# Products of 1024 columns from two PSUM banks, and attention scores in the projections' banks

## The chip, the cores and the metric

The kernel runs on one core of one Trainium2 chip. The metric is the time of one execution on the device, in microseconds (us). A core has five engines that work side by side, each through its own instructions in order: TensorE (PE, matmuls; its weight loads are shown apart as PEld), VectorE (DVE), ScalarE (ACT), GpSimd (POOL) and SyncE (SP), which here issues the loads. Matmuls write to PSUM, which this kernel uses as eight banks of 128 partitions by 512 fp32 columns.

## The reference

Two layers act on 256 latent tokens of width 2048, with 256 context tokens beside them; all is fp32. From the conditioning vector c each layer makes a shift, a scale and a gate, three vectors of 2048 values, with one large matrix (2048 by 6144 per layer). Cut to what matters here:

```python
sc = silu(c)
for layer in range(2):
    mod = sc @ ada_w[layer] + ada_b[layer]           # 6144 values
    shift, scale, gate = split(mod, 3)
    h = rmsnorm(x, norm_g[layer]) * (1 + scale) + shift
    if layer == 0:
        k, v, q, za, glu, zb = split(h @ w_in)       # context tokens give k and v too
        q, k = rope(rmsnorm(q)), rope(rmsnorm(k))    # 8 query heads, 2 key/value heads, 128 wide
        s = q @ k.T * 128 ** -0.5                    # 256 queries, 512 keys
        attn = softmax(s) @ v
        conv = silu(layernorm(depthwise_conv_31(glu)))
        x = x + gate * (concat(attn * silu(za), conv * silu(zb)) @ w_out)
    else:
        u, v, z = split(h @ od_w_in)                 # gated position mixing
        x = x + gate * ((gelu(u) * mix(layernorm(gelu(v))) * silu(z)) @ od_w_out)
out = rmsnorm(x, final_g)
```

## The kernel before, in words

**Jobs.** All weights are streamed from memory once, in blocks of 128 partitions by up to 1024 columns (512 KB). A block is a job: its load goes to one of ten ring buffers (tag `raw`), 12 jobs ahead of its use. A weight job is then split into a high and a low part, the high one by ACT (L358), the low one by POOL or VectorE (L361), and enters matmuls in three products (L383, L385, L386 where features lie on partitions; L406 to L408 where tokens do) that accumulate in one PSUM bank. A gate projection (`z_part`) has four groups of 96 such matmuls; ACT takes each out of its bank with a SiLU (L588). There are two gate projections, z0 and z1.

**The conditioning vectors.** One part of `ada_w` goes over TensorE. For eight blocks of 1024 output columns (TSET), c alone is needed, and these go over VectorE, in `adat_jobs`: the matrix is stored transposed, output columns on partitions, and a job multiplies a block elementwise with c and sums along the row (L269, a product with an accumulator; the trace shows the accumulator's read as an operation of its own). c, copied over all partitions, lies in SBUF as `cb` (2048 columns); `cb_part` has ACT copy 512 columns of it to a PSUM bank (`cbp`, L248), from which VectorE reads it. A block has 16 jobs in four column ranges q of 512; each job holds two sets of 128 output columns (k = 0, 1) and makes two products of 512 columns. After four jobs ACT fills the bank with the next range. Blocks run through the ranges alternately upwards and downwards, so that one filling serves two of them. The partial sums land in `res` and are added by L277. Four of the eight blocks are used in layer 0's stretch of the program, four in layer 1's.

**PSUM.** Every tile in PSUM is one bank with a tag: three banks for the projections' accumulators (`acc`, tag a), one for the attention scores (`S`, tag s), one for `cbp` (tag c), and three for everything else (tag m: the convolution, the transposes, the attention output and the sums).

**Attention.** For each of 16 heads and query blocks, `attn_head` makes the scores in S (L755, 128 queries by 512 keys), VectorE takes the maximum from S (L758), ACT the exponential from S (L761), VectorE scales the result (L766). `attn_tr` transposes it on TensorE (L775), `attn_pv` multiplies four heads with the values (L783), and ACT copies that out (L787). S is held from its matmul to the end of its exponential. The convolution's 31 taps per channel block are VectorE operations into PSUM (L613).

**The order.** The program lists the jobs in a plan; conditioning jobs are woven between weight jobs, and the steps of attention and convolution are handed out after each weight job at a set pace. The scheduler of the language then orders each engine's instructions by their place in the program and by a simulation of their times; a tile gets a bank when one of its tag is free in that simulation. On the chip every engine keeps that order, and waits at the instruction whose inputs or bank are not ready.

Of the kernel before, what the change touches and what calls it, by code (L numbers as in the profile page):

```python
# [11 lines left out]
F32 = mybir.dt.float32  # L12
F32R = mybir.dt.float32r
AF = mybir.ActivationFunctionType
ALU = mybir.AluOpType
AX = mybir.AxisListType

D = 2048
NKB = 16
T = 256  # L20
# [15 lines left out]
SMALL_W = _off  # L36
BANKS = {"acc": "a", "S": "s", "conv": "m", "ada": "m", "cbp": "c"}
BUFS = {'a': 3, 's': 1, 'm': 3, 'c': 1}
ZG = ()
# [20 lines left out]
RW = 10  # L60
# [22 lines left out]
def backbone_kernel(  # L83
# [21 lines left out]
    nc = tc.nc  # L105
# [8 lines left out]
    def ld(dst, src):  # L114
        """a load, in the order of the program."""
        i = nc.sync.dma_start(dst, src)
        cnt[0] += 1
        return tc.keep_in_program_order(i) if cnt[0] <= NL else i
# [46 lines left out]
    def bcast(dst, n, hi=rowh, lo=rowl, k=10):  # L165
        """row n over all partitions; dst in PSUM."""
        nc.tensor.matmul(dst, sel[0:k, n : n + 1].broadcast_to([k, 128]), hi, start=True, stop=False)
        nc.tensor.matmul(dst, sel[0:k, n : n + 1].broadcast_to([k, 128]), lo, start=False, stop=True)
# [16 lines left out]
    def colsum(p, ones, src, n, tot):  # L185
        """partial sums over the partitions of block n of tot, in the column tile n % 4 of the PE array."""
        g = n % 4
        nc.tensor.matmul(p[32 * g : 32 * g + 32, :T], ones, src, start=n < 4, stop=n >= tot - 4, tile_position=(0, 32 * g))  # L188

    def colsum_all(p):  # L190
        """the four partial sums added, on every partition, in PSUM."""
        r = tmp.tile([128, T], F32, tag="adar", name="csum", bufs=1)
        nc.scalar.copy(r, p[:, :T])
        o = bank("csum_p")
        nc.tensor.matmul(o[:, :T], q4, r, start=True, stop=True)
        return o

    def colsum_rstd(p):
        """1 / sqrt(the four partial sums added + eps) of each token, on every partition, in PSUM."""
        r = tmp.tile([128, T], F32, tag="adar", name="csum", bufs=1)  # L200
# [14 lines left out]
    def warm(func):  # L215
        """loads the table of func ahead of its use."""
        tc.keep_in_program_order(nc.scalar.activation(wrm, epsc, func))
# [12 lines left out]

# [1 line left out]
    modv = [con.tile([128, 3, NKB], F32, name=f"modv{i}") for i in range(2)]  # L232
    modc = con.tile([128, 2, NKB], F32, name="modc")

    class Job:
        raw = None
# [7 lines left out]
    def cb_part(q):  # L244
        """columns 512 q .. of cb to PSUM."""
        if cbq["q"] != q:
            cbq["q"], cbq["t"] = q, bank("cbp")
            nc.scalar.copy(cbq["t"], cb[:, q * 512 : (q + 1) * 512])  # L248

    def adat_jobs(l, c0):  # L250
        """1024 columns for c alone, columns on partitions, on the vector engine."""
        js = []
        n = TSET.index((l, c0))
        res = tmp.tile([128, 8, 4], F32, tag="adat", name="adat", bufs=2)
        order = range(4) if n % 2 == 0 else range(3, -1, -1)
        for u, q in enumerate(order):
            for t in range(4):
                jb = Job()
                jb.kind = "A"

                def load(jb=jb, t=t, q=q):
                    jb.raw = ring.tile([128, 2, 512], F32, tag="raw", name="traw", bufs=RW)
                    ld(jb.raw, adat_d[n, q, t].rearrange("p (a b) -> p a b", a=2))

                def mm(jb=jb, t=t, q=q, u=u):
                    cb_part(q)
                    with after("crit"):
                        for k in range(2):
                            nc.vector.scalar_tensor_tensor(  # L269
                                out=jb.raw[:, k, :], in0=jb.raw[:, k, :], scalar=1.0, in1=cbq["t"], op0=ALU.mult,  # L270
                                op1=ALU.mult, accum_out=res[:, 2 * t + k, q : q + 1])
                    if t == 3 and u < 3:
                        cb_part(order[u + 1])
                    if t == 3 and u == 3:
                        kind, k0 = c0 // D, (c0 % D) // 128
# [10 lines left out]
    def adan_jobs(l, c0, cw, slot=1):  # L286
        """columns c0 .. c0 + cw of a layer's adaLN projection, four column tiles of the PE array at a time;
        rows 32 g and 32 g + 1 of the result are c and c_ctx, for a part of the columns (or of the k-blocks)."""
        js = []
# [52 lines left out]

# [1 line left out]
    def w_job(src, width, mmf, tot=1024):  # L344
        """src: [128, tot] block in DRAM, width: columns of a k-row."""
        jb = Job()
# [20 lines left out]
    def w_rows(jobs, src, kbs, h, post):  # L367
        """features on partitions: [128 of 2 blocks, tokens]; src[kq] is the block of 4 k-blocks."""
        accs = {}
# [21 lines left out]
    def w_cols(jobs, src_f, kbs, hs, post):  # L391
        """tokens on partitions: hs = list of (h, chunk); src_f(kp) gives the block of 2 k-blocks."""
        parts = [(kp, [kb % 2 for kb in kbs if kb // 2 == kp]) for kp in sorted({kb // 2 for kb in kbs})]
# [26 lines left out]

# [1 line left out]
    def rms_rB(src_half, name):  # L422
        """rstd of each token over D, broadcast over partitions."""
        pr = bank("rms")
        for i in range(2):
            sq = s8("sq")
            nc.scalar.activation(sq, src_half[i], AF.Square)
            if i == 1:
                warm(AF.Sqrt)
            for k in range(8):  # L430
                colsum(pr, onesD, sq[:, k, :], i * 8 + k, 16)
        rB = tmp.tile([128, T], F32, tag="rB", name=name, bufs=2)
        nc.scalar.copy(rB, colsum_rstd(pr))
        return rB
# [5 lines left out]
    def make_h(src_f, rB, shift, scale, hh, hl, kbs, m=8, rP=None, mh=0):  # L440
        """hh/hl [128, 8, T] pieces for the k-blocks kbs (2 at a time)."""
        prev = None
# [20 lines left out]

# [1 line left out]
    zT = {}  # L465
# [43 lines left out]
    def weave(a, b):  # L509
        """b spread evenly through a."""  # L510
        out, n = [], 0
# [12 lines left out]
    def part(dst, a, g):  # L524
        """partial sum over a K group into dst."""
        if g == 0:
# [4 lines left out]
    def kv_part(kqs):  # L531
        """keys (cg 0) and values (cg 1) of x and of the context over some K: [128 tokens of two chunks, 256]."""
        js = [hook(lambda kq=kq: prep_c(kq)) for kq in kqs]
# [42 lines left out]
    def z_part(which, g=None):  # L576
        """SiLU gates; over one K group when g is given, else over all of K."""
        js = []
# [16 lines left out]

# [1 line left out]
    TAPS = [PAD] + [t for t in range(CW) if t != PAD]  # L597

    def conv_taps(i, t0, t1):
        """taps t0 .. t1 (of TAPS) of channel block i; the first covers every token."""  # L600
        if i % 2 == 0 and t0 == 0:
# [69 lines left out]

# [1 line left out]
    knb = con.tile([128, 128], F32, name="knb")  # L673
# [18 lines left out]
    def rope(dst, src, nm, c, nh):  # L692
        """dst, src: [128, nh, 128] (even half, odd half)."""
        def tb(n):
# [23 lines left out]
    def rope_k(i):  # L718
        """rows of keys: chunks 0,1 latent (rotated), 2,3 context."""
        if "kT" not in at:  # L720
# [87 lines left out]

# [1 line left out]
    def hm(kb):  # L810
# [3 lines left out]
    def out_part(w, l, h, fin, kbs, last):  # L814
        """x += gate * (h @ w) over the k-blocks kbs."""
        segs = []
# [14 lines left out]

# [1 line left out]
    l1 = {}  # L833
# [35 lines left out]
    def v_part(g):  # L869
        """half the K of v; with the second half its statistics and norm."""  # L870
        js = []
# [40 lines left out]
    def sgu(i):  # L912
        """mixed positions of channel blocks 2i, 2i+1 (one group) times u."""
        pm = bank("sgu")
# [63 lines left out]

# [1 line left out]
    def need(key):  # L980
# [112 lines left out]
def _layout(i):  # L1093
# [25 lines left out]
    def xt(x):  # L1119
# [6 lines left out]
        "ada": np.concatenate([a["ada_w"][l][:, c : c + 256] for l, c in NCOLS], axis=1),  # L1126
        "adat": np.stack([a["ada_w"][l][:, c : c + 1024].T.reshape(4, 2, 128, 4, 512).transpose(3, 0, 2, 1, 4).reshape(4, 4, 128, 1024)
                          for l, c in TSET]),
# [23 lines left out]
```

## Time and profile before

| | |
|---|---|
| time, median of 3 runs | 936.31 us (932.75 to 938.0) |
| profiled execution: its span | 928.0 us, first to last instruction |
| median of the runs less that span | 8.3 us |
| TensorE busy in the span | 869.7 us (94%) |
| VectorE busy | 684.8 us (74%) |
| ScalarE busy | 456.1 us (49%) |
| GpSimd busy | 256.1 us (28%) |
| read from memory | 235.80 MB, 256 GB/s over the span |
| mean granted TensorE clock | 0.979 of full speed |

The profile is of one execution; its span leaves out what lies before the first and after the last instruction. Lines of groups read: source line, engine, operation, output<-inputs by the program's names with their shapes, count | busy us, mean ns of one | idle time of the engine just before them, and what ended most of it. Lines in order of time begin with the start and the duration in us; a bracket at the end tells how long the engine had stood idle and what released it. Lines of stretches give the stretch, its length, each engine's busy time with the number of instructions, the granted clock, the DMA share and GB/s.

### The profile page before, as it was taken

The numbers are of one execution on the slowest core, as the hardware profiler recorded it, in microseconds if no ns is written. First come the engines' busy times: TensorE is split into PE (matmuls) and PEld (weight loads), VectorE is DVE, ScalarE is ACT, GpSimd is POOL, SyncE is SP. The second block draws the span as 40 slices with busy tenths as digits, with TensorE's granted clock in tenths as the row PEclk, the third lists the DMA queues.
The fourth block names the chain that finished last, engine by engine and source line by source line (L and its number), as shares of the span: only waits on it lengthen the run. The fifth ranks groups of instructions, "written<-read, shape, count | busy, mean of one in ns | idle before, by whom it ended". The sixth has DMA issues, their size and how long they took to land.

```text
span 928.0 us, 17854 instructions
## 1 busy us (share of the span) xinstructions
PE 869.7 (94%) x7052; PEld 793.0 (85%) x7052; DVE 684.8 (74%) x1432; ACT 456.1 (49%) x650; POOL 256.1 (28%) x111
## 2 busy tenths in 40 slices
PE   5899999898987999998989899999999999999995
PEld 3788999897766987788979778998899999999994
DVE  1365565889999999987796289889989877654443
ACT  4544132464644755554654454555474444444441
POOL 0000014567856544556687630000000000000000
PEclk9899999999989999999999999999999999999998
DMA  9999989855776844667869689998987888755502
GB/s 320 374 387 354 332 300 360 315 205 142 244 275 203 281 151 135 221 199 236 300 227 367 207 289 399 375 333 287 312 304 228 252 273 273 229 183 176 165 1 90
DMA packets 79152, 239.05 MB, mean 258 GB/s; under 512 B 7503, under 2 KB 15961, under 8 KB 78557
## 3 DMA queue, kind: packets, MB, share of 16 engines
q1 hardware_dynamic: 79068, 237.92, 75.0%
q8 instruction: 55, 0.90, 0.4%
q14 instruction: 29, 0.23, 0.1%
HBM read 235.80 MB, written 2.10 MB: 256 GB/s over the span
## 4 chain that ended last, share of the span: by engine, by line
PE 51%; DVE 5%; DMA 2%; ACT 1%; issue 1%; POOL 0%; DVEq 0%; POOLq 0%
PE acc L386 13%; PE acc L385 13%; PE acc L383 12%; PE acc L406 3%; PE acc L407 3%; PE acc L408 3%; DMA traw<-adat 2%; DVE traw L269 1%; DVE conv L613 1%; PE rms L188 1%; PE sgu L918 1%; DVE P L766 1%; DVE gaT L645 1%; DVE mBl L438 1%; ACT whi L358 0%
## 5 line engine op out<-in xcount | busy, mean ns | idle before, releaser
L358 ACT ACTIVATE whi<-raw 128x1024 fp32r<-128x1024 f32 (+1 forms) x256 | 263.5, 1031 | 287.7 <-PE acc L385 131.9
L361 POOL TENSOR_TENSOR wlo<-raw,whi 128x1024 fp32r<-128x1024 f32 x104 | 254.9, 2459 | 293.8 <-ACT whi L358 280.7
L361 DVE TENSOR_TENSOR wlo<-raw,whi 128x1024 fp32r<-128x1024 f32 (+1 forms) x152 | 176.9, 1165 | 103.6 <-ACT whi L358 102.7
L269 DVE SCALAR_TENSOR_TENSOR traw<-traw,cbp 128x512 f32<-128x512 f32 x256 | 165.0, 680 | 37.3 <-DMA traw<-adat 30.6
L383 PE MATMUL acc<-h,whi 128*128 128x256 f32 x512 | 150.6, 296 | 1.9 <-ACT h L453 1.9
L385 PE MATMUL acc<-h,whi 128*128 128x256 f32 x512 | 150.4, 295 | 1.9 <-DVE h L457 1.9
L386 PE MATMUL acc<-h,wlo 128*128 128x256 f32 x512 | 146.9, 288 | 0.0
L383 PE MATMUL acc<-h1h,whi 128*128 128x256 f32 x512 | 145.3, 284 | 0.0
L385 PE MATMUL acc<-h1l,whi 128*128 128x256 f32 x512 | 144.9, 283 | 0.0
L386 PE MATMUL acc<-h1h,wlo 128*128 128x256 f32 x512 | 144.6, 283 | 0.0
L613 DVE SCALAR_TENSOR_TENSOR conv<-gaT,small,conv 128x242 f32<-128x242 f32 (+14 forms) x240 | 107.7, 472 | 1.8
L383 PEld LDWEIGHTS acc<-h,whi 128*128 128x128 f32 x512 | 99.0, 194 | 8.2 <-issue 3.7
L385 PEld LDWEIGHTS acc<-h,whi 128*128 128x128 f32 x512 | 99.1, 194 | 6.6 <-issue 4.0
L386 PEld LDWEIGHTS acc<-h,wlo 128*128 128x128 f32 x512 | 99.0, 194 | 3.5 <-issue 3.5
L383 PEld LDWEIGHTS acc<-h1h,whi 128*128 128x128 f32 x512 | 98.2, 192 | 0.1
L385 PEld LDWEIGHTS acc<-h1l,whi 128*128 128x128 f32 x512 | 98.3, 192 | 0.1
L386 PEld LDWEIGHTS acc<-h1h,wlo 128*128 128x128 f32 x512 | 98.1, 192 | 0.0
L386 PE MATMUL acc<-m1h,wlo 128*128 128x256 f32 x256 | 73.1, 286 | 0.0
L383 PE MATMUL acc<-m1h,whi 128*128 128x256 f32 x256 | 72.4, 283 | 0.0
L385 PE MATMUL acc<-m1l,whi 128*128 128x256 f32 x256 | 72.4, 283 | 0.0
L386 PEld LDWEIGHTS acc<-m1h,wlo 128*128 128x128 f32 x256 | 49.1, 192 | 2.9 <-issue 2.9
L407 PE MATMUL acc<-wlo,h1h 128*128 128x512 f32 x128 | 50.7, 396 | 0.0
(230 smaller groups left out, 1667.5 us busy)
## 6 DMA issues: line engine op xcount, KB each, us to landing
traw<-adat SPq DMA_DIRECT2D x128, 512.0 KB, 4.7
raw<-w_out SPq DMA_DIRECT2D x64, 512.0 KB, 4.3
raw<-w_uz SPq DMA_DIRECT2D x64, 512.0 KB, 4.7
araw<-ada SPq DMA_DIRECT2D x56, 512.0 KB, 7.7
raw<-w_gate SPq DMA_DIRECT2D x56, 512.0 KB, 5.0
raw<-w_v SPq DMA_DIRECT2D x32, 512.0 KB, 5.2
raw<-w_q SPq DMA_DIRECT2D x16, 512.0 KB, 3.7
raw<-w_gate SPq DMA_DIRECT2D x16, 256.0 KB, 8.7
```

Of the source, the lines that this page charges most:

```text
L188: nc.tensor.matmul(p[32 * g : 32 * g + 32, :T], ones, src, start=n < 4, stop=n >= tot - 4, tile_position=(0, 32 * g))
L269: nc.vector.scalar_tensor_tensor(out=jb.raw[:, k, :], in0=jb.raw[:, k, :], scalar=1.0, in1=cbq["t"], op0=ALU.mult, op1=ALU.mult, accum_out ...
L358: nc.scalar.activation(hv, jb.raw, AF.Copy)
L361: eng.tensor_tensor(out=jb.lo.rearrange("p a b -> p (a b)"), in0=jb.raw, in1=hv.bitcast(F32), op=ALU.subtract)
L383: nc.tensor.matmul(o, wh, hh, start=(n == 0 and kt == kts[0] and b == 0), stop=False, skip_group_check=True)
L385: nc.tensor.matmul(o, wh, hl, start=False, stop=False, skip_group_check=True)
L386: nc.tensor.matmul(o, wl, hh, start=False, stop=end, skip_group_check=True)
L406: nc.tensor.matmul(accs[i], hh[:, sl], jb.hi[:, k, :], start=s0, stop=False)
L407: nc.tensor.matmul(accs[i], hh[:, sl], jb.lo[:, k, :], start=False, stop=False)
L408: nc.tensor.matmul(accs[i], hl[:, sl], jb.hi[:, k, :], start=False, stop=s1)
L438: return nc.vector.tensor_tensor(out=lo, in0=src, in1=hi.bitcast(F32), op=ALU.subtract)
L613: nc.vector.scalar_tensor_tensor(out=o, in0=y, scalar=w, in1=o, op0=ALU.mult, op1=ALU.add)
```

## The change

The layout of the eight transposed blocks on the host becomes two column ranges of 1024 with eight jobs each in place of four ranges of 512 with four; a job is the same 512 KB. `cbp` becomes a tile of two banks, filled by two copies of 512 columns, and a job is one product of 1024 columns. `res` has two partial sums per output in place of four. To free a bank, the tag s goes and S takes its bank from tag a, which keeps three. The diff without removed comments:

```diff
-BANKS = {"acc": "a", "S": "s", "conv": "m", "ada": "m", "cbp": "c"}
-BUFS = {'a': 3, 's': 1, 'm': 3, 'c': 1}
+BANKS = {"acc": "a", "S": "a", "conv": "m", "ada": "m", "cbp": "c"}
+BUFS = {'a': 3, 'm': 3, 'c': 1}
...
     def cb_part(q):
         if cbq["q"] != q:
-            cbq["q"], cbq["t"] = q, bank("cbp")
-            nc.scalar.copy(cbq["t"], cb[:, q * 512 : (q + 1) * 512])
+            cbq["q"], cbq["t"] = q, psum.tile([128, 1024], F32, tag="c", name="cbp", bufs=1)
+            for x in range(2):
+                nc.scalar.copy(cbq["t"][:, x * 512 : (x + 1) * 512], cb[:, q * 1024 + x * 512 : q * 1024 + (x + 1) * 512])
...
-        res = tmp.tile([128, 8, 4], F32, tag="adat", name="adat", bufs=2)
-        order = range(4) if n % 2 == 0 else range(3, -1, -1)
+        res = tmp.tile([128, 8, 2], F32, tag="adat", name="adat", bufs=2)
+        order = range(2) if n % 2 == 0 else range(1, -1, -1)
         for u, q in enumerate(order):
-            for t in range(4):
+            for t in range(8):
...
-                    jb.raw = ring.tile([128, 2, 512], F32, tag="raw", name="traw", bufs=RW)
-                    ld(jb.raw, adat_d[n, q, t].rearrange("p (a b) -> p a b", a=2))
+                    jb.raw = ring.tile([128, 1024], F32, tag="raw", name="traw", bufs=RW)
+                    ld(jb.raw, adat_d[n, q, t])
...
-                        for k in range(2):
-                            nc.vector.scalar_tensor_tensor(
-                                out=jb.raw[:, k, :], in0=jb.raw[:, k, :], scalar=1.0, in1=cbq["t"], op0=ALU.mult,
-                                op1=ALU.mult, accum_out=res[:, 2 * t + k, q : q + 1])
-                    if t == 3 and u < 3:
+                        nc.vector.scalar_tensor_tensor(
+                            out=jb.raw, in0=jb.raw, scalar=1.0, in1=cbq["t"], op0=ALU.mult,
+                            op1=ALU.mult, accum_out=res[:, t, q : q + 1])
+                    if t == 7 and u < 1:
                         cb_part(order[u + 1])
-                    if t == 3 and u == 3:
+                    if t == 7 and u == 1:
...
-        "adat": np.stack([a["ada_w"][l][:, c : c + 1024].T.reshape(4, 2, 128, 4, 512).transpose(3, 0, 2, 1, 4).reshape(4, 4, 128, 1024)
+        "adat": np.stack([a["ada_w"][l][:, c : c + 1024].T.reshape(8, 128, 2, 1024).transpose(2, 0, 1, 3)
                           for l, c in TSET]),
```

## The prediction

> **What bounds the kernel now.** I read the busy times of the page first, then the busy times of three long stretches, then the groups of VectorE, the waits, and the order of time where the scores are made. The page's span and first section:
>
> ```profile
> span 928.0 us, 17854 instructions
> ...
> PE 869.7 (94%) x7052; PEld 793.0 (85%) x7052; DVE 684.8 (74%) x1432; ACT 456.1 (49%) x650; POOL 256.1 (28%) x111
> ```
>
> TensorE (PE) is busy 94% of the span, so as a whole the kernel is bound by matmuls. VectorE (DVE), where the edit is, can move the end only in a stretch in which PE waits. Three stretches, with the columns PE, PEld, DVE, ACT, POOL, granted clock, DMA share and GB/s:
>
> ```profile
> 200.00:412.00 212.00, 192.65 (x1233) 167.05 (x1233) 203.79 (x476) 119.94 (x200) 127.00 (x53) 0.97 0.62 202
> 412.00:540.00 128.00, 118.71 (x897) 106.84 (x895) 86.82 (x200) 64.08 (x87) 83.26 (x35) 0.97 0.76 258
> 540.00:800.00 260.00, 259.98 (x1835) 244.45 (x1834) 223.43 (x444) 137.90 (x166) 6.81 (x3) 1.00 0.89 306
> ```
>
> From 540 to 800 us (layer 1) PE never stops. Whatever VectorE saves there is hidden by the matmuls. From 200 to 412 us (queries, rotary, attention, convolution taps) it is the other way round: VectorE is busy 203.8 of 212 us and PE shows 19 us of idle time. This stretch is where the edit is worth anything. From 412 to 540 us VectorE has 41 us of slack and PE 9.
>
> **The change part by part: the products.** A job of 512 KB is now two products of 512 columns; it becomes one of 1024. The groups of VectorE between 200 and 412 us, and the product's group between 412 and 540 us:
>
> ```profile
> L613 DVE SCALAR_TENSOR_TENSOR conv<-gaT,small,conv 128x242 f32<-128x242 f32 (+14 forms) x213 | 94.8, 472 | 1.3
> L269 DVE SCALAR_TENSOR_TENSOR traw<-traw,cbp 128x512 f32<-128x512 f32 x60 | 39.0, 677 | 1.7 <-DMA traw<-adat 1.0 <-ACT PT L776 0.7
> ```
> ```profile
> L269 DVE SCALAR_TENSOR_TENSOR traw<-traw,cbp 128x512 f32<-128x512 f32 x57 | 36.7, 681 | 19.2 <-DMA traw<-adat 16.1 <-issue 1.9 <-ACT whi L358 1.1
> ```
>
> 60 products are 30 jobs in the stretch that counts, and 57 are about 28 jobs in the next. What a product takes from its neighbours is the distance between starts, since the shown ends overlap the next start. VectorE in order of time, a job at 241 us and a 1024-column subtraction at 701 us:
>
> ```profile
> 241.34 0.68 DVE L269 SCALAR_TENSOR_TENSOR traw<-traw,cbp 128x512 f32<-128x512 f32 x1
> 241.94 0.08 DVE L269 DVE_READ_ACCUMULATOR traw<-traw,cbp 128x1 f32 x1
> 241.94 0.68 DVE L269 SCALAR_TENSOR_TENSOR traw<-traw,cbp 128x512 f32<-128x512 f32 x1
> ```
> ```profile
> 701.58 1.22 DVE L361 TENSOR_TENSOR wlo<-raw,whi 128x1024 fp32r<-128x1024 f32 x1
> 702.72 0.69 DVE L931 TENSOR_TENSOR m<-m,mixed 128x512 f32<-128x512 f32 x1
> ```
>
> Two products take 2 x 0.605 = 1.21 us. The accumulator's read starts with the next operation, so halving the number of reads gains nothing. No row shows a product of 1024 columns. It cannot be worse than two of 512 unless a read across two banks is slower, for which no row speaks: 1.21 us, no gain. The nearest row is the subtraction of the same width, 702.72 - 701.58 = 1.14 us. I take 1.135, so a job gains 0.075 us. In 200 to 412 us that is 30 x 0.075 = 2.2 us, all on the engine that bounds. In 412 to 540 us it is 28 x 0.075 = 2.1 us, but there VectorE stood 16.1 us waiting for the products' own loads, and a shorter product then only waits longer; I take half, 1.0 us. In layer 1 it is nothing, by the cover above; without that cover 61 jobs would be worth 4.6 us. Bounds of this part: 0 and 9.6 us (128 jobs).
>
> [...]
>
> **The conditioning copies and the loads.** ScalarE's (ACT's) group of copies over the whole span:
>
> ```profile
> L248 ACT COPY cbp<-cb 128x512 f32<-128x512 f32 x25 | 14.8, 592 | 22.4 <-DVE traw L269 22.4
> ```
>
> By the code the 25 fillings of one bank become 9 of two, so 18 copies of 0.59 us. ACT is busy 120 of 212 us, which covers them. Its waits for a product, which hold up what follows it on ACT, are in the waits between 200 and 420 us:
>
> ```profile
> ACT cbp L248 <- DVE traw L269: 12.5, 3, 8.8
> PE qtp L748 <- DVE qr L704: 12.2, 2, 6.8
> ```
>
> The 8.8 us wait lies beside a PE wait of 6.8 us for VectorE's rotary output (qr), which ACT does not feed, so taking it away releases nobody: 0, with up to 3 us if the shorter waits counted. Against it, the first product behind a switch now waits for two copies, 0.59 us more at each of 5 switches before 540 us: at most 3 us of loss. Loads stay 128 issues of 512 KB on SP's queue. I take 0 for all of it.
>
> **The scores.** S had a bank of its own; now it takes one of the three that the projections use. What the single bank costs: the scores' weight loads after 300 us, then PE and ACT in order of time.
>
> ```profile
> L755 PEld LDWEIGHTS S<-kT,qT x28: 186/192/192, 305.9 to 398.9; 128*128 128x128 f32 x28
> ```
> ```profile
> 308.37 0.28 PE L383 MATMUL acc<-h,whi 128*128 128x256 f32 x1
> ...
> 360.05 0.29 PE L383 MATMUL acc<-h,whi 128*128 128x256 f32 x1
> ...
> 368.18 1.13 PE L755 MATMUL S<-kT,qT 128*128 128x512 f32 x2 [1.22 <-ACT P L761]
> ...
> 378.42 0.28 PE L383 MATMUL acc<-h,whi 128*128 128x256 f32 x1
> ...
> 384.58 1.02 PE L755 MATMUL S<-kT,qT 128*128 128x512 f32 x2
> ```
> ```profile
> 310.11 0.60 ACT L588 ACTIVATE z0T<-acc 128x512 f32<-128x512 f32 x1
> ...
> 367.94 0.19 ACT L761 ACTIVATION_READ_ACCUMULATOR P<-S,mx,qss 128x1 f32 x1
> ...
> 382.00 0.19 ACT L761 ACTIVATION_READ_ACCUMULATOR P<-S,mx,qss 128x1 f32 x1
> ...
> 386.49 0.59 ACT L787 COPY mixA<-O 128x512 f32<-128x512 f32 x1 [3.35 <-PE O L783]
> ...
> 388.38 1.09 ACT L588 ACTIVATE z1T<-acc 128x512 f32<-128x512 f32 x2
> ```
>
> 28 loads are 14 heads, one every (398.9 - 305.9) / 13 = 7.1 us. The head at 368.18 starts as soon as the exponential before it is through with the bank (367.94 + 0.19). Where only one projection is open, S could now have a second bank. The wait of 1.22 us is the largest that PE shows there; I take it as gained once, 1.2 us (bounds 0 and the 6.9 us worked out below).
>
> What the missing bank costs: a gate group holds its bank through its 96 matmuls and then until ACT has made its SiLU. I counted groups of 96 from the first gate matmul: the third begins at 308.37, the sixth at 360.05, the seventh at 378.42. At 308.37 the first two gate groups wait for ACT (the earlier is out at 310.11 + 0.60) and a score is open, so all three banks would be taken: 2.3 us of wait. At 378.42 the groups before it are let go together at 388.38 + 1.09, because ACT's order puts them behind the third attention output (mixA at 386.49). The third bank then holds the score until 382.2, 3.8 us, and the score of 384.58 finds none until 389.0, 4.4 us. Behind a waiting matmul stands all of PE's order: more gate matmuls, the transposes of P, and behind these VectorE's maximum and ACT's exponential. Together 10.5 us. VectorE has taps and products queued meanwhile, and it is VectorE that bounds, so I take 3 us (bounds 0 and the 13.9 worked out below).
>
> **The sum.** -2.2 - 1.0 - 1.2 + 3 = -1.4 us. The profiled execution's span of 928.0 us lies 8.3 us below the median of the runs, 936.3; applied to the median, the sum gives 935, and I put 934, because the second bank's bound is open on the gaining side. The scheduler builds each engine's order from its own simulation, so operations will also change places. The price of that can only be bounded: VectorE's operations with two SBUF inputs do not take the same time everywhere.
>
> ```profile
> L701 DVE TENSOR_TENSOR qr<-rp,rp 128x256 f32<-128x256 f32 x4 | 6.3, 1582 | 0.0
> ```
>
> Four of one shape average 1.58 us, while 512 columns were shown at 0.68 to 0.69 in the rows above. So 4 us hang on where such a group falls. That makes about 5 us either way.
>
> **Rivals.** *Attention runs ahead (faster).* If S mostly has two banks, heads no longer follow one another at 7.1 us, the taps (94.8 us of VectorE) slide behind attention, where VectorE has its 41 us of slack, and PE's idle time there goes. Busy times:
>
> ```profile
> 280.00:300.00 20.00, 15.19 (x122) 14.51 (x121) 20.00 (x36) 8.88 (x13) 13.17 (x6) 0.96 0.59 188
> 300.00:320.00 20.00, 18.02 (x130) 17.09 (x131) 18.57 (x54) 13.04 (x19) 9.84 (x5) 0.87 0.88 308
> 300.00:420.00 120.00, 113.12 (x770) 96.32 (x770) 110.78 (x268) 71.93 (x103) 62.41 (x26) 0.98 0.61 201
> ```
>
> PE is idle 120 - 113.1 = 6.9 us from 300 to 420. With the products' 3.2 us that is 926 us. For it: the heads stand in a row behind one bank. Against it: VectorE is 110.8 of 120 us busy there and its order is fixed before the run, so a score that is early may only wait longer for its maximum.
>
> *The shared bank decides (slower).* All 10.5 us fall on PE's path, as the gate matmuls that PE cannot do before 420 us have to be done later, where it has little idle time. A PE wait like those for qr is followed by a lower clock: 0.96 and 0.87 in the two rows above, (0.04 + 0.13) x 20 = 3.4 us of lost matmul time. Then 10.5 + 3.4 - 3.2 gives about 947 us. It decides as soon as more than some 4 us of bank waits reach PE's path. For it: 29 us pass from the end of the fifth gate group, where the sixth begins (360.05), to its release at 389. Against it: the scheduler may start the gates' SiLU earlier when banks are short.
>
> [...]
>
> *The change does not shorten anything.* A product across two banks takes 1.21 us, or VectorE waits for loads instead: 936 us. This lies inside the forecast.
>
> **How the numbers follow.** The forecast, 934, has 0.46, with its own range 929 to 940. The faster rival has 0.30, the slower one 0.24. About 0.5% (4.7 us) is what a measurement of this kernel tells from no change. Of the forecast's 0.46, 0.34 lies within that, 0.07 below and 0.05 above. Of the faster rival 0.28 is below, of the slower one 0.22 above, and 0.02 of each within. That makes 0.35 faster, 0.38 the same, 0.27 slower. The range starts 6 us below the faster rival's price, about what the order may move, and ends at the slower one's, which has counted every wait in full: 920 to 947.
>
> **What would show it.** Products: 128 of 1024 columns, starts 1.13 to 1.14 us apart; 1.21 or more means no gain. Copies: 18, and fewer ACT waits for products. Scores: starts less than 7.1 us apart, with no start on the heels of an exponential, would be the faster rival. A PE wait for ACT's SiLU or exponential ahead of a gate matmul, or a clock below 0.95 between 300 and 420 us, would be the slower one. Layer 1, 540 to 800 us, should keep its length. If it doesn't, the prediction's cover is wrong. If attention ends more than 5 us from 412 us, my sum missed the main term.

## The result: 1.1% slower

The median after is 943.71 us (940.56 to 945.51) against 934.53 us for the kernel before beside it (931.3 to 939.48), six runs each. The ratio is 1.011, with a 95% interval of 1.0084 to 1.0136 (the two medians alone give 1.0098). Two of the twelve runs of one kernel below, before6_kr, were over 1.5% above its fastest, and its median and ratio leave them out. The forecast was 934 us with its own range up to 940. The time lies outside that, and inside the wide range that ended at 947.

The profiled execution of after has a span of 940.9 us and a time of 942.68 us. Its span is 12.9 us above that of before, while the medians are 9.2 us apart. So some 3.7 us of what the two traces show apart is the quick execution that was profiled before, and no reading below hangs on a difference that small.

The first section of after's page, then three stretches (columns PE, PEld, DVE, ACT, POOL, granted clock, DMA share, GB/s):

```profile
span 940.9 us, 17649 instructions
...
PE 880.5 (94%) x7052; PEld 799.6 (85%) x7052; DVE 683.9 (73%) x1176; ACT 453.4 (48%) x643; POOL 257.5 (27%) x111
```
```profile
200.00:412.00 212.00, 189.43 (x1143) 159.80 (x1143) 201.14 (x416) 116.52 (x196) 117.81 (x49) 0.94 0.55 183
412.00:540.00 128.00, 121.48 (x957) 111.79 (x956) 80.49 (x129) 62.11 (x81) 93.57 (x38) 0.99 0.80 279
540.00:800.00 260.00, 258.12 (x1756) 239.95 (x1757) 221.94 (x323) 134.51 (x163) 7.12 (x3) 0.98 0.87 298
```

Most of the loss lies between 200 and 412 us. PE's idle time there went from 212 - 192.65 = 19.3 to 212 - 189.43 = 22.6 us, which is 3.2 us. The granted clock fell from 0.97 to 0.94, which is about 0.03 x 212 = 6.4 us of full-speed matmul time. Together that is 9.6 us. From 412 to 800 us the same sum gives -0.9 us of idle time and, from the clocks, -2.6 + 5.2 us: some 2 us more. (The clocks are rounded to 0.01, so such a product can be off by some 2 us.)

The product itself did what was predicted. VectorE of after in order of time shows starts 1.14 us apart, where two halves took 1.21:

```profile
546.09 1.22 DVE L269 SCALAR_TENSOR_TENSOR traw<-traw,cbp 128x1024 f32<-128x1024 f32 x1
547.23 0.09 DVE L269 DVE_READ_ACCUMULATOR traw<-traw,cbp 128x1 f32 x1
547.23 1.22 DVE L269 SCALAR_TENSOR_TENSOR traw<-traw,cbp 128x1024 f32<-128x1024 f32 x1
```

So VectorE has less to do and PE waits longer for it. The larger waits of PE in after, 200 to 440 us (what waited, for what: us in total, times, longest):

```profile
PE qtp L748 <- DVE qss L221: 5.8, 2, 3.8
PE qtp L748 <- DVE qr L704: 3.7, 1, 3.7
PE ktp L735 <- DVE kr L732: 3.4, 1, 3.4
PE ktp L735 <- DVE kr L704: 3.2, 2, 2.0
PE qtp L748 <- DVE mx L762: 2.6, 1, 2.6
PE acc L383 <- ACT P L761: 1.8, 1, 1.8
PE S L755 <- ACT P L761: 1.3, 1, 1.3
```

The last two are the waits for a shared bank, 3.1 us in all. The others are waits for VectorE, 18.7 us, all of them ahead of 412 us, where before has 16.7 us. The 3.4 us for the last key block (kr, L732) did not exist before. VectorE around it, first before, then after:

```profile
221.52 0.99 DVE L732 TENSOR_TENSOR kr<-kv_sb,knb 128x256 f32<-128x256 f32 x1
...
224.30 1.03 DVE L664 TENSOR_TENSOR gaT<-gaT,gbT 128x512 f32<-128x512 f32 x1
225.25 0.97 DVE L613 SCALAR_TENSOR_TENSOR conv<-gaT,small,conv 128x244 f32<-128x244 f32 x2
226.14 1.74 DVE L732 TENSOR_TENSOR kr<-kv_sb,knb 128x256 f32<-128x256 f32 x1
```
```profile
223.39 2.00 DVE L732 TENSOR_TENSOR kr<-kv_sb,knb 128x256 f32<-128x256 f32 x1
...
226.20 2.01 DVE L664 TENSOR_TENSOR gaT<-gaT,gbT 128x512 f32<-128x512 f32 x1
228.13 1.48 DVE L613 SCALAR_TENSOR_TENSOR conv<-gaT,small,conv 128x243 f32<-128x243 f32 x3
229.64 0.55 DVE L611 TENSOR_SCALAR conv<-gaT,small 128x256 f32<-128x256 f32 x1
230.23 0.98 DVE L613 SCALAR_TENSOR_TENSOR conv<-gaT,small,conv 128x241 f32<-128x241 f32 x2
231.12 1.94 DVE L732 TENSOR_TENSOR kr<-kv_sb,knb 128x256 f32<-128x256 f32 x1
```

In VectorE's order of before 29 convolution taps stand ahead of the last key block, in that of after 34. The key block comes 5.0 us later. Five taps, some 0.45 us each from start to start, are 2.2 us of that. Another 2.0 us are two operations that last a microsecond longer each than before: the key block ahead (2.00 for 0.99 us) and L664 (2.01 for 1.03 us); no run here shows why they do. What the delay does to PE, whose next instruction is the key's transpose, stands in PE's order of time in after:

```profile
228.82 0.39 PE L408 MATMUL acc<-whi,h 128*128 128x512 f32 x1
229.05 0.61 PE L406 MATMUL acc<-whi,h 128*128 128x512 f32 x2
233.11 0.69 PE L735 MATMUL ktp<-ident,kr 128*128 128x128 f32 x2 [3.44 <-DVE kr L732]
...
234.02 0.63 PE L408 MATMUL acc<-whi,h 128*128 128x512 f32 x1
234.45 0.63 PE L406 MATMUL acc<-whi,h 128*128 128x512 f32 x1
```

PE stands for 3.44 us, and then its matmuls start 0.43 us apart instead of 0.23, until about 236.2 us: half speed for some 3 us (the granted clock is 0.50 from 233.11 to 236.20 us), 1.5 us of lost work. This place costs about 5 us. Waits with slower matmuls behind them come again in attention, where the twenty-microsecond stretches of after give:

```profile
280.00:300.00 20.00, 16.05 (x95) 13.67 (x93) 19.75 (x33) 9.74 (x24) 9.80 (x4) 0.83 0.63 220
300.00:320.00 20.00, 15.57 (x86) 12.09 (x87) 17.52 (x43) 12.74 (x20) 5.27 (x3) 0.83 0.57 195
```

Before, these rows had clocks of 0.96 and 0.87.

### The profile page after: what moved, and what is told of

Its sections match the earlier page's. It is cut to its first block, busy times and chain, and to the rows that moved or that the text cites. A ratio compares the mean times of both kernels' runs of the same rounds, so it can differ in the third digit from the quotient of the medians.

```text
span 940.9 us, 17649 instructions
## 1 busy us (share of the span) xinstructions
PE 880.5 (94%) x7052; PEld 799.6 (85%) x7052; DVE 683.9 (73%) x1176; ACT 453.4 (48%) x643; POOL 257.5 (27%) x111
## 4 chain that ended last, share of the span: by engine, by line
PE 68%; DVE 17%; DMA 6%; issue 4%; POOL 3%; ACT 2%; SPq 0%; DVEq 0%; POOLq 0%; ACTq 0%
PE acc L383 16%; PE acc L386 16%; PE acc L385 15%; DVE traw L269 4%; PE ada L314 3%; DVE conv L613 3%; DMA traw<-adat 3%; PE acc L408 3%; POOL wlo L361 3%; PE acc L406 3%; PE acc L407 3%; PE acc L548 1%; PE O L783 1%; PE acc L550 1%; PE acc L552 1%
## 5 line engine op out<-in xcount | busy, mean ns | idle before, releaser
L361 POOL TENSOR_TENSOR wlo<-raw,whi 128x1024 fp32r<-128x1024 f32 x104 | 256.4, 2475 | 302.0 <-ACT whi L358 276.6
L361 DVE TENSOR_TENSOR wlo<-raw,whi 128x1024 fp32r<-128x1024 f32 (+1 forms) x152 | 177.1, 1167 | 109.8 <-ACT whi L358 108.4
L269 DVE SCALAR_TENSOR_TENSOR traw<-traw,cbp 128x1024 f32<-128x1024 f32 x128 | 154.9, 1215 | 47.0 <-DMA traw<-adat 37.7
L408 PE MATMUL acc<-whi,h1l 128*128 128x512 f32 x128 | 51.0, 404 | 1.9 <-DVE h1l L457 1.9
```

The lines of the kernel that those rows point to most:

```text
L269: nc.vector.scalar_tensor_tensor(out=jb.raw, in0=jb.raw, scalar=1.0, in1=cbq["t"], op0=ALU.mult, op1=ALU.mult, accum_out=res[:, t, q : q + 1])
L361: eng.tensor_tensor(out=jb.lo.rearrange("p a b -> p (a b)"), in0=jb.raw, in1=hv.bitcast(F32), op=ALU.subtract)
L408: nc.tensor.matmul(accs[i], hl[:, sl], jb.hi[:, k, :], start=False, stop=s1)
```

## The experiments

Ratios are to the kernel before, run on the same chip in the same batch; its medians were 933.0, 934.4, 933.8 and 934.1 us. In the edited kernels line numbers are up to three higher than in after.

**One part at a time.** The first two kernels are before with the scores in the projections' tag, once with three banks (one PSUM bank stays unused) and once with four:

```diff
-BANKS = {"acc": "a", "S": "s", ...}
-BUFS = {'a': 3, 's': 1, 'm': 3, 'c': 1}
+BANKS = {"acc": "a", "S": "a", ...}
+BUFS = {'a': 3, 'm': 3, 'c': 1}      # share3_512
+BUFS = {'a': 4, 'm': 3, 'c': 1}      # share4_512
```

> The scores in the projections' three banks, products of 512 columns from one bank as before (one bank of PSUM stays unused). Theory A, the place of the scores in the order: with a second bank open to them, the scheduler puts attention ahead of the gate matmuls, these then stand behind waits for VectorE and behind a low clock; then this kernel has the whole of layer 0's loss, +9 us, 943 to 944 us, a granted clock of 0.94 from 200 to 412 us, and none of the 3.8 us lost at the border between the layers. Theory B, the width: long products hold up what stands behind them on VectorE; then this kernel takes 934 to 936 us.

> As the run before it, but four banks for projections and scores together, so that no bank is missing. Theory A1 (the scores' early place in the order costs, whatever the number of banks): +6 to +12 us, 941 to 946 us, as the scores stand even earlier in PE's order. Theory A2 (the bank that is missing costs): no loss, 932 to 935 us. Theory B (width): 934 to 936 us.

The third is after, with S in a bank of its own again and two banks left for the projections:

```diff
-BANKS = {"acc": "a", "S": "a", ...}
-BUFS = {'a': 3, 'm': 3, 'c': 1}
+BANKS = {"acc": "a", "S": "s", ...}
+BUFS = {'a': 2, 's': 1, 'm': 3, 'c': 1}
```

> Products of 1024 columns from two banks, the scores in a bank of their own, the projections with two banks in place of three. The scores stand in PE's order where they stood before. Theory A: layer 0's loss of 9 us is gone; with the products' gain of some 3 us and the 3.8 us at the border about 935 us, more if two banks are too few for the projections (a PE wait for ACT's SiLU then shows). Theory B: 940 to 944 us, as the long products are all there.

share3_512 took 936.20 us, ratio 1.0029 (1.0008 to 1.005); share4_512 930.23 us, 0.9975 (0.9951 to 0.9999); wide_a2 953.74 us, 1.0218 (1.0186 to 1.025). Sharing alone gains 2.7 us with four banks and costs 3.2 us with three. The bank that the wide product takes is therefore worth some 6 us, more than the 3 us of the prediction. But sharing with three banks explains only a third of the loss, since it costs 0.3% and after 1.1%. With two banks for the projections the loss is larger than either theory expected. It no longer ends with layer 0, as the row of wide_a2 for layer 1 shows, 7.8 us of idle time where before had none:

```profile
540.00:800.00 260.00, 252.20 (x1672) 231.26 (x1673) 215.38 (x316) 130.40 (x160) 9.19 (x4) 0.97 0.84 288
```

In share4_512 the one long wait for a bank did appear (200 to 440 us):

```profile
PE acc L383 <- ACT P L761: 6.7, 1, 6.7
PE qtp L748 <- DVE qr L704: 5.4, 1, 5.4
```

Before waited 12.2 us for qr, in two waits. Here 6.7 + 5.4 = 12.1 us are one wait for a bank and one for qr, and the kernel is no slower. So a bank wait of this length need not be a loss: PE stood as long as it had stood for VectorE.

**The width alone.** after_split is after in all, banks and layout and loads, except that a job makes two products of 512 columns, one from each bank of `cbp`:

```diff
-                        nc.vector.scalar_tensor_tensor(
-                            out=jb.raw, in0=jb.raw, scalar=1.0, in1=cbq["t"], ..., accum_out=res[:, t, q : q + 1])
+                        for x in range(2):
+                            s = slice(x * 512, (x + 1) * 512)
+                            nc.vector.scalar_tensor_tensor(out=jb.raw[:, s], in0=jb.raw[:, s], scalar=1.0,
+                                in1=cbq["t"][:, s], ..., accum_out=res[:, t, 2 * q + x : 2 * q + x + 1])
```

> The changed kernel in everything (two banks for c, ranges of 1024 columns, scores in the projections' banks), but each job's product is made as two of 512 columns, one per bank. If the width of the products is what costs beyond sharing (4 us at the border by the run with the raised bound, some 3.5 us in layer 0): 936 to 937 us, as with sharing alone, and no PE wait for the fifth low part at the border. If the two-bank fill, the longer ranges or their copies cost: 941 to 944 us.

It took 935.77 us, ratio 1.0008 (0.9986 to 1.0031). So 943.71 - 935.77 = 7.9 of after's 9.2 us (the medians of before in the two batches, 934.5 and 934.4, agree) hang on the width of one instruction that is itself 0.07 us a job quicker. VectorE of after_split has the key block where before had it, behind 29 taps:

```profile
226.10 1.75 DVE L734 TENSOR_TENSOR kr<-kv_sb,knb 128x256 f32<-128x256 f32 x1
```

No product stands on VectorE between 197 and 244 us in after, so the wide product does not block the key block. What remains is the scheduler's simulation, in which one longer instruction in place of two lets five more taps go ahead; that is inferred from the two orders and not shown. The width doesn't do this beside any banks: wide_a2 has 29 taps there too. Its key block comes as late as after's (231.67 us) for another reason, which isn't shown, and PE has no wait for it, so lateness alone is not the loss either.

**The border to layer 1.** In after five products stand in one row ahead of a low part of layer 1's input (h1l, L457), 5.7 us, and PE waits for a later one:

```profile
544.95 1.22 DVE L269 SCALAR_TENSOR_TENSOR traw<-traw,cbp 128x1024 f32<-128x1024 f32 x1
...
549.51 1.22 DVE L269 SCALAR_TENSOR_TENSOR traw<-traw,cbp 128x1024 f32<-128x1024 f32 x1
549.51 0.08 DVE L269 DVE_READ_ACCUMULATOR traw<-traw,cbp 128x1 f32 x1
550.66 1.00 DVE L457 SCALAR_TENSOR_TENSOR h1l<-ht,modv,h1h 128x256 fp32r<-128x256 f32 x1
```
```profile
558.16 0.39 PE L408 MATMUL acc<-whi,h1l 128*128 128x512 f32 x1
560.43 0.59 PE L408 MATMUL acc<-whi,h1l 128*128 128x512 f32 x1 [1.88 <-DVE h1l L457]
```

The five products are not all of it: between them and that wait the two operations of L924 last 2.79 us, where before has 0.61 us, and two of L457 last 3.03 us, where before has 0.88 us; no run here shows why.

The products are held behind the first feature blocks of a modulation up to a bound, CR. Three kernels raise that bound for layer 1's first modulation, so that all eight of its blocks come ahead of the products. They are after, before, and share4_512 with:

```diff
-    def make_h(src_f, rB, shift, scale, hh, hl, kbs, m=8, rP=None, mh=0):
+    def make_h(src_f, rB, shift, scale, hh, hl, kbs, m=8, rP=None, mh=0, cr=CR):
...
-            if k0 <= kbs[0] + CR:
+            if k0 <= kbs[0] + cr:
...
-               range(g * 8, g * 8 + 8), rP=rP, mh=MH if g == 0 else 0)
+               range(g * 8, g * 8 + 8), rP=rP, mh=MH if g == 0 else 0, cr=6 if g == 0 else CR)
```

> The changed kernel, but in layer 1's first modulation the products stand behind all eight k-blocks in place of the first four (the bound of the rule that already holds them back is raised from 2 to 6). Theory B for the border (five products of 1024 columns stand ahead of the fifth low part, 5.7 us in place of 3.0 us): the PE wait of 1.88 us for it and the low clock behind it go, 943.7 - 3.8 = 940 us. If the border's loss is only carried over from layer 0: 943 to 944 us.

> The kernel before with the raised bound alone (products behind all eight k-blocks in layer 1's first modulation). If products of 512 columns cost nothing at the border because five of them take 3.0 us: 932 to 934 us, no change. If the bound is worth its 4 us whatever the width: 929 us.

> Sharing with four banks, products of 512 columns, and the raised bound. 930 us as with four banks alone if the bound is worth nothing at that width, 926 us if it is worth 4 us.

after_cr6 took 939.69 us, 1.0069 (1.0044 to 1.0095), so 4 us seem to have come back, though the interval overlaps that of after (from 1.0084). before_cr6 took 933.62 us, 0.9996 (0.997 to 1.0023), no change. share4_cr6 took 931.27 us, 0.9959 (0.9937 to 0.998), which is as fast as share4_512 without the raised bound (930.23 us). That looked like a cost of the wide product at the border. The last experiment speaks against that.

**The heads in a row.** One theory was that S with several banks lets the scores come too early, and that this costs. share3_chain is share3_512 with each head's scores made to depend on the exponential of the head before, as a single bank would force it:

```diff
+        mm = nc.tensor.matmul(S, at["qT"]..., at["kT"]..., start=True, stop=True)
+        if "exp" in at:
+            tc.add_manual_dep(mm.ins, at["exp"].name, ...)
...
+        at["exp"] = nc.scalar.activation(P, S, AF.Exp, bias=mx[:, 1:2], scale=rq, accum_out=mx[:, 2:3]).ins
```

> Sharing alone as before (three banks, products of 512 columns), but each head's score matmul waits for the exponential of the head before it, so that the scores never hold two of the three banks. If the second bank taken from the projections is what sharing costs (+3 us with three banks, -2 us with four): 930 to 933 us. If it is where the scheduler puts the operations: no clear change from 936, 934 to 939 us.

It took 947.19 us, 1.015 (1.0113 to 1.0188), which is 11 us more than share3_512 and more than either case had expected. The theory fell: with the scores in a row the kernel is slower, and share4_512, whose last attention output starts at 395.0 us against 412.4 before, is not slower. The loss stands in the stretches around the first heads, where PE is idle for 17.9 of 40 us at clocks of 0.75 and 0.65. In share3_512 it is idle for 11.1 us there, at clocks of 0.90 and 0.84. The rows of share3_chain:

```profile
280.00:300.00 20.00, 9.82 (x54) 7.10 (x52) 19.57 (x56) 7.31 (x11) 6.95 (x3) 0.75 0.77 247
300.00:320.00 20.00, 12.29 (x49) 8.56 (x49) 19.01 (x56) 9.08 (x14) 0.68 (x1) 0.65 0.32 99
```

**The key block ahead of the taps.** If the order at the last key block is what the width spoils, then a kernel in which the taps cannot pass it should get the width's gain. Taps that the program lists after the last key block are held behind it. (The line edited makes the last two key blocks, so taps listed after the third are held behind that one too: 20 stand ahead of it, where before has 24 and after 26.)

```diff
-            nc.vector.tensor_tensor(out=kr, in0=s3, in1=knb..., op=ALU.mult)
+            at["krl"] = nc.vector.tensor_tensor(out=kr, in0=s3, in1=knb..., op=ALU.mult).ins
...
-            if n == 0:
-                nc.vector.tensor_scalar(out=o, ...)
+            with tc.issue_after(at["krl"]) if "krl" in at else nullcontext():
+                if n == 0:
+                    nc.vector.tensor_scalar(out=o, ...)
```

Four kernels have this beside the raised border: after, after_split, before, and share4_512. The fifth is after with this edit alone.

> The changed kernel with the raised bound, and with the convolution's taps that the program lists behind the last key block (from the fourth block's scaled key on) held behind it in VectorE's order: 24 taps then stand ahead of it, in place of 34 with wide products and 29 with narrow ones. If the rest of the width's loss (939.7 against 935.8 with two halves, some 5 us more by the landmarks of layer 0) comes from this one place, where PE waits 3.4 us for that key and then runs at half clock: 934 to 936 us, and within 0.3% of the next run. If it comes from long products standing ahead of other work all through layer 0: 938 to 941 us.

> The same two holds with each job's product made as two of 512 columns. Compared with the run before it, only the width of the products differs, with the same 24 taps ahead of the last key. One place: within 0.3% of the run before it, or that one faster by the products' 2 to 3 us. All through layer 0: this one faster by 3 us or more, 933 to 936 us against 938 to 941.

> The kernel before with the same two holds: what they are worth without the change. The wait for the last key was 0.4 us or less there, so 931 to 935 us, no change.

> Four shared banks, products of 512 columns, with both holds. 931 us as without the second hold; 927 us if the earlier key also shortens the wait for the first rotated queries.

> The changed kernel with the taps held behind the last key, without the raised bound. If the border between the layers costs its 4 us of itself, as the run with the raised bound alone made it (943.7 to 939.7 us): 932 to 933 us against 928.7 with both. If the border's loss hung on what came before it: 928 to 930 us. The first hold is worth 943.7 - 932.5 = 11 us in the one case, 15 in the other.

| kernel | median, us | ratio to before (95%) | taps ahead of the last key block |
|---|---|---|---|
| after6_kr (wide, three banks) | 928.66 | 0.9941 (0.9922 to 0.996) | 24 |
| after_kr (the same, border as it was) | 928.67 | 0.9948 (0.9922 to 0.9974) | 24 |
| split6_kr (two halves, three banks) | 931.77 | 0.999 (0.9972 to 1.0007) | 24 |
| share4_6kr (two halves, four banks) | 930.04 | 0.9962 (0.9943 to 0.9981) | 24 |
| before6_kr (before, both edits) | 932.6 | 0.9996 (0.9972 to 1.0021) | 24 |

The hold brings the wide kernel from 943.7 to 928.7 us, 15 us, which is more than was expected of it in either case. It leaves before where it was (932.6 us beside 933.8). The kernel with two halves goes from 935.77 to 931.77 us with both edits, 4 us, by intervals that overlap. So the hold is worth nothing to before, and what it mends in the wide kernel, some 11 to 15 us, is an order that came with the width. The waits of PE in after_kr, 200 to 440 us, are nearly those of before (12.2 us for qr there), and the wait for L732's key block (L733 here) is gone:

```profile
PE qtp L749 <- DVE qr L705: 11.3, 2, 6.7
PE S L756 <- ACT P L762: 2.1, 2, 1.9
PE ktp L736 <- DVE kr L705: 2.0, 1, 2.0
```
```profile
200.00:412.00 212.00, 196.50 (x1248) 169.83 (x1247) 200.43 (x439) 123.50 (x205) 126.25 (x52) 0.95 0.61 199
412.00:540.00 128.00, 122.19 (x914) 109.97 (x913) 78.73 (x136) 63.85 (x90) 87.21 (x37) 0.97 0.81 280
540.00:800.00 260.00, 258.09 (x1835) 243.10 (x1834) 219.06 (x311) 133.51 (x157) 4.67 (x2) 1.00 0.87 301
```

From 200 to 412 us PE does 7.1 us more work than in after, at a clock 0.01 higher. The border's rows of waits show the same thing again on a smaller scale: between 520 and 570 us PE waits for h1l 1.9 us at once in after, and here

```profile
PE acc L408 <- DVE h1l L457: 1.1, 2, 0.9
```

with a clock of 1.00 behind it. after_kr and after6_kr, without and with the raised border, have the same time, though five wide products stand ahead of the same low part in after_kr as well (531.00 to 536.70 us). So the five wide products have no price of their own that shows. What of the 4 us of after_cr6 was real, and what of it came over from layer 0, stays open.

In the held order the width alone is worth 931.77 - 928.66 = 3.1 us, and the two intervals do not overlap. The lost bank, together with the new ranges, costs 931.77 - 930.04 = 1.7 us, with intervals that do overlap, so it is not told from nothing there.

## Why the prediction was wrong

**What bounds the kernel: right.** Most of the loss and of the repair lies between 200 and 412 us, where VectorE is busy 201 of 212 us.

**The products: right in size.** -2.2 and -1.0 us were predicted from the 0.075 us of a job. The trace shows 1.14 us for 1.21, and in the held order the width is worth 3.1 us against the 3.2 of the sum. That they agree to 0.1 us is luck, as each of the two ratios is known to some 2 us.

**Copies and loads: right.** The copies are 18 in the trace of after, and its waits of PE between 200 and 440 us name neither a copy nor a load. after_split has the same copies and loads and takes 935.77 us, no more than sharing alone.

**The banks: sign right, place not.** The sum had -1.2 us for a second bank of the scores and +3 for the missing one, +1.8 together. Sharing with three banks cost 3.2 us (936.20 against 932.96), by its interval 0.7 to 4.7 us, so 1.8 may well be right. But the three places that the prediction named, 2.3 + 3.8 + 4.4 us, did not come. after's bank waits are 1.8 us ahead of its fourth gate group (347.48 us) and 1.3 us at a score (301.11 us); its gate matmuls no longer stood where the places had been read. The slower rival ended at 947 us and the time was 944, but that it came so near is luck. Its first sign was there, the wait for an exponential ahead of a gate matmul (1.8 us). Its second was not, a clock below 0.95 between 300 and 420 us: after has 0.96 over that stretch, and 0.83 in the first row, where before already had 0.87. Its mechanism carries some 5 us at most: 3.1 us of waits, and behind the longer one clocks of 0.91 and 0.75 in the two rows of 5 us from 345 to 355 us, (0.09 + 0.25) x 5 = 1.7 us. The wait of 3.44 us for VectorE at 233 us has half speed behind it as well (0.50), so a low clock does not tell the two apart.

**The order: the step that failed.** The prediction said that operations would change places, put "about 5 us either way" on it, and left its centre at zero. It took that size from the rotary group's uneven durations, a matter of one group of VectorE operations. The runs show that the order is worth 15 us to the wide kernel, some 11 of them beyond what the same hold gives with two halves. Five more taps ahead of the last key block, together with two operations that lasted longer, put a wait of 3.4 us and a stretch at half clock on PE, and attention behind it came in another order with waits of its own. How the 10 us beyond the first 5 divide among those later places isn't shown, because the hold that removes the first also changes the rest. The uneven durations that the prediction named were a part of it (2.0 of the 5.0 us by which the key block came late), but a price taken from VectorE alone left out what PE loses behind one late operation.

That the place is sensitive could have been read from before, where PE already waited for the key blocks ahead of the last one, and 29 taps stood ahead of that:

```profile
PE ktp L735 <- DVE kr L704: 2.7, 2, 1.6
```

What could not have been read is that five more would go through. The sign of the term could not be known, but the bound of 5 us was too narrow: one more wait like that of 3.44 us, with 1.5 us lost at half clock behind it, is already 5 us, and such places exist at each key and query block.

**Attention runs ahead: the mechanism came, the gain did not.** The attention outputs (O) of before and of after, first and last start:

```profile
L783 PE MATMUL O<-PT,kv_sb x32: 590/592/594, 331.0 to 412.4; 128*128 128x512 f32 x32
```
```profile
L783 PE MATMUL O<-PT,kv_sb x32: 590/592/1061, 323.6 to 408.0; 128*128 128x512 f32 x32
```

Attention ended 4.4 us earlier in the slower kernel. PE had put gate matmuls off and had them still to do: counted in groups of 96, the second group starts at 310.3 us where before had 285.9, and the ninth at 426.4 where before had 415.0. The end of attention was a bad sign to watch: the prediction's 5 us around 412 did not trip, and the sum had missed its main term all the same.

**Layer 1.** The cover held for the products, but 540 to 800 us did not keep its full speed: 1.9 us idle and a clock of 0.98. The idle time is the wait for h1l. after_kr's row has the same idle time with a clock of 1.00, and after6_kr, which waits for no h1l there, has the same median. So the cover failed by a wait whose price by itself is not told from nothing. The clock's part in after is a half-clock stretch behind that wait (0.59 from 560 to 564 us), and the one at the border between the layers, which lies behind 540 us here (0.83 from 540 to 560 us) and lay ahead of it in before (0.83 from 520 to 540 us).

## What to carry to other kernels

Where a scheduler builds each engine's order from simulated times, a change to one instruction can change the order far from where it stands (here inferred from the two orders), and one misplaced dependency can cost more than the change saves. So look for the first PE wait that the kernel before did not have, count what stands ahead of its producer in both orders, and hold that producer in place before judging the change: here this turned 1.1% slower into 0.5 to 0.6% faster, after_kr being the simplest kernel that is faster than both before and after. A long wait for a bank is no price in itself, as share4_512 shows (one of 6.7 us, in a kernel no slower than before), until it is known what PE would have waited for otherwise.

## What the runs showed of the hardware

**A wait of 1.88 us cost nearly twice its length.** PE's wait of 1.88 us for h1l in after, at 558.55 us, is followed by this (stretches of 4 us):

```profile
556.00:560.00 4.00, 2.55 (x12) 1.77 (x10) 4.00 (x5) 1.06 (x1) 2.53 (x2) 1.00 0.99 384
560.00:564.00 4.00, 3.57 (x9) 2.80 (x10) 2.72 (x5) 1.18 (x2) 0.09 (x1) 0.59 0.50 179
564.00:568.00 4.00, 4.00 (x19) 3.28 (x18) 3.44 (x6) 3.06 (x4) 0.00 (x0) 0.99 0.94 350
```

A clock of 0.59 over 4 us is 1.6 us of lost work behind a wait of 1.88 us. It is not always so: behind a wait of 2.01 us that ended at 261.6 us in after the clock stayed full,

```profile
261.60:266.00 4.40, 4.38 (x22) 3.71 (x23) 4.40 (x7) 1.65 (x2) 2.34 (x2) 1.00 0.70 238
```

and no run here shows what tells the two apart. The wait of 3.44 us, quoted above, had a stretch of about 3 us at half clock (0.50) behind it. The clock between 200 and 412 us was lower in after, with several waits of 2 to 4 us (0.94), than in before, with two of 5.4 and 6.8 us (0.97). The prediction, which priced a clock loss only in its slower rival, and there from the two rows around the wait of 6.8 us, missed that.

**A product over two PSUM banks took no longer than an operation of the same width from SBUF.** Products of 1024 columns from two banks start 1.14 us apart in after, and the subtraction of the same width from SBUF (L361) takes 1.14 us to the next start in before (701.58 to 702.72 us). Their shown lengths in after are 1.22 us each, so the boundary between the banks costs nothing that shows.
